# The first projection of a two-block network on one core: order of the modulation vector's copies, loads in flight, parts of the contraction, and which engine keeps the partial sums

## Chip, cores and metric

One core of a Trainium2 chip runs the whole program in one launch. The metric is device time in microseconds (us), lower is better. The times of the kernel before are three runs; the profile is one more execution.

## What is computed

Two transformer blocks follow each other on a sequence of 256 tokens with 2048 channels, in fp32. The change lies in the start of the first:

```python
mod = jax.nn.silu(c) @ w_ada[l] + b_ada[l]
shift1, scale1, gate1, shift2, scale2, gate2 = jnp.split(mod, N_MOD, axis=-1)
h = rms_norm(x, norm1_w[l]) * (1.0 + scale1[:, None]) + shift1[:, None]
proj = h @ w_in[l]
u_pool, q, k, v, g_a, g_b = jnp.split(proj, split_at, axis=-1)
```

`c` is one vector of 2048, `w_ada` is 2048 x 12288, `w_in` 2048 x 8192. Column k of `h` (128 channels, 16 such columns) can be made only when 128 values of `scale1` and 128 of `shift1` are known, and each of these groups of 128 costs one product of a 1 MB piece of `w_ada` with `c`. So the first projection needs 32 such products, and contracts over column k once column k is there.

## The kernel before

**Stream of blocks.** All weights of the large products pass as *blocks* of 1 MB (`raw`, 128 x 4 x 512 floats): four *units*, each 128 contraction rows by 512 output columns. A block has two halves of two units. For each half ScalarE rounds to fp32r (`hi`, L201), VectorE subtracts to get the rest (`lo`, L209), and TensorE makes per unit and per half of the tokens three matmuls of 512 columns (hi x hi L303, lo x hi L304, hi x lo L305): 24 matmuls a block. Four buffers hold `hi`, four `lo`, four `raw`. `Net.run` prepares halves three ahead of the one whose matmuls it issues; a half's `hi` waits until TensorE has finished the half four before it.

**Modulation products.** `ada_product` (L177) multiplies one 1 MB piece of `w_ada` with `cb` (silu(c) on all partitions) and sums along the row, on VectorE: one column of `mod`. Pieces stand in the same queue as the blocks; `pump` keeps at most `ADAB` = 2 loaded and not yet used. `prep_hi` takes the products and calls that stand ahead of a block just before that block's first `hi`.

**Start.** `setup` copies c in, applies silu and spreads it by four fp32 matmuls (L495) over four PSUM tiles. `block1` then, for each of two token halves, takes the sum of squares on ScalarE (L541), the reciprocal root (`rstd`, L335 to L340), and scales x on VectorE (L543); after the first half VectorE copies the four PSUM tiles to `cb` (L546). x is turned by 32 transposes (L555) with eight copies on ScalarE (L556).

**A column of h.** `h_tile(k)` follows the second product of column k: two one-column operations on VectorE (`sAB`, L561 and L563), then `modulate`: ScalarE writes the rounded half (L382), VectorE the full value (L383) and the difference (L384). In ScalarE's queue the next block's `hi` comes right behind L382.

**Order of the first 48 blocks.** `startup_blocks` (STARTUP = 48) orders 12 groups of 512 output columns (four of `ga`, two each of `q`, `k`, `u`, `v`) against parts of the contraction. CHUNKS = (0, 4, 10, 16): first columns 0 to 3 for all groups (blocks 0 to 11), then 4 to 9 (12 to 29), then 10 to 15 (30 to 47). `ga` 0 and 1 keep their sums in PSUM all the way; the other ten groups hold a pair of PSUM tiles (tag `acc`, four in all, two groups at a time) for one part, and `part_end` takes the sums out at the part's end: copied by ScalarE after the first part (L605), added on VectorE after the others (L607). The dictionary `when` places the products: two ahead of each of the first four blocks, then 12 from block 5 on, 1.1 blocks apart, then 12 from block 19.5 on, 1.05 apart. Behind block 47 comes `w_a_up` (its matmuls read `pT`).

Of the kernel before, what the change touches and what calls it, by code (L numbers as in the profile page):

```python
# [8 lines left out]
F32 = mybir.dt.float32  # L9
# [4 lines left out]
AF = mybir.ActivationFunctionType  # L14
# [4 lines left out]
P = 128  # L19
D = 2048  # L20
# [9 lines left out]
HLB = 4  # L30
LOOK = 3
ADAB = 2


_PK = {}
# [10 lines left out]
class Seg:  # L46
# [5 lines left out]
    def __init__(self, lhs, ks, end=None, tag="acc", end_tt=None, tail=2):  # L52
        self.lhs, self.ks, self.end, self.tag, self.end_tt = lhs, list(ks), end, tag, end_tt
        self.tail = tail if end_tt else 0
        self.acc = None
        self.left = [len(self.ks)] * 2


def lag(n):
# [4 lines left out]
class Net:  # L64
# [92 lines left out]
    def pump(self):  # L157

        while self.q_dma < len(self.queue):
            kind, what, src = self.queue[self.q_dma]  # L160
            if kind == "w":
                if what - self.prepped // 2 >= RAWB:
                    return
                t = self.rawp.tile([P, 4, 512], F32, tag="raw", name="raw")
                self.nc.sync.dma_start(out=t, in_=src)
                self.raw[what] = t
            elif kind == "a":
                if len(self.ada_dma) - self.ada_done >= ADAB:
                    return
                t = self.adap.tile([P, D], F32, tag="ada", name="ada")  # L170
# [122 lines left out]

    def unit(self, seg, k, hi, lo, tts=(0, 1)):
        if seg.acc is None:
            seg.acc = [self.psp.tile([P, 512], F32, tag=seg.tag, name="acc") for _ in range(2)]
        for tt in tts:
            first = seg.left[tt] == len(seg.ks)
            seg.left[tt] -= 1
            last = seg.left[tt] == 0  # L300
            xh, xl = seg.lhs(k, 0, tt), seg.lhs(k, 1, tt)
            a = seg.acc[tt]
            self.nc.tensor.matmul(a, xh, hi, start=first, stop=False)  # L303
            self.nc.tensor.matmul(a, xh, lo, start=False, stop=False)  # L304
            self.nc.tensor.matmul(a, xl, hi, start=False, stop=last)  # L305
# [176 lines left out]
    def setup(self):  # L482
# [22 lines left out]
        self.mask = self.t2([P, P], name="mask")  # L505
        nc.sync.dma_start(out=self.mask, in_=A["mask"])
# [5 lines left out]
        nc.vector.memset(self.eps, EPS)  # L512
        self.mod1 = fix.tile([P, 96], F32, tag="mod1", name="mod1")
        self.mod2 = fix.tile([P, 96], F32, tag="mod2", name="mod2")

    def setup2(self):
        nc, fix = self.nc, self.fix
# [8 lines left out]
    def block1(self):  # L526
# [13 lines left out]
        for tt in range(2):  # L540
            nc.scalar.activation(junk, x[:, tt, :], AF.Square, accum_out=tot[:, tt:tt + 1])  # L541
            r = self.rstd(tot[:, tt:tt + 1], 1, D)
            nc.vector.tensor_scalar(out=x[:, tt, :], in0=x[:, tt, :], scalar1=r, scalar2=None, op0=ALU.mult)  # L543
            if tt == 0:
                for i, ps in enumerate(self.cbps):
                    nc.vector.tensor_copy(self.cb[:, i * 512:(i + 1) * 512], ps)  # L546
        nc.vector.scalar_tensor_tensor(out=wb, in0=self.pk("b_ada", 16, 16), scalar=1.0, in1=self.pk("norm1_w"),
                                       op0=ALU.add, op1=ALU.mult)
        xT = mp.tile([P, KD, S], F32, tag="B", name="xT")

        for tt in range(2):
            for c in range(4):
                ps = self.ms([P, 4, P])
                for i in range(4):
                    nc.tensor.transpose(ps[:, i, :], x[:, tt, (4 * c + i) * P:(4 * c + i + 1) * P], self.ident)  # L555
                nc.scalar.copy(xT[:, 4 * c:4 * c + 4, tt * P:(tt + 1) * P], ps)  # L556
        self.at(6, self.setup2)
# [68 lines left out]
        chunk = {}  # L626
        ch = CHUNKS

        when = {}
        for c, (b0, every) in enumerate(((5, 1.1), (19.5, 1.05)), 1):  # L630
            for i in range(2 * (ch[c + 1] - ch[c])):
                when.setdefault(int(b0 + every * i), []).append((ch[c] + i // 2, i % 2))
        for nb, bl in enumerate(startup_blocks()):
            if nb < ch[1]:
                need(nb)
            for k, i in when.get(nb, ()):
                self.add_ada(ada[16 * i + k])
                if i:
                    self.add_call(lambda k=k: h_tile(k))
            units = []  # L640
            for key, k in bl:
                c = max(i for i in range(len(ch)) if ch[i] <= k)
                if key not in held and (key, c) not in chunk:
                    chunk[key, c] = Seg(h_lhs, range(ch[c], ch[c + 1]), part_end(key, c))
# [791 lines left out]


STARTUP = 48
CHUNKS = (0, 4, 10, 16)


def startup_blocks():
# [4 lines left out]
    for c in range(len(ch) - 1):  # L1447
# [2 lines left out]
            out += [(g, k) for k in ks for g in keys[:4]]  # L1450
            rest = keys[4:]
        else:
            rest = [keys[i] for i in (2, 3, 4, 0, 5, 1, 6, 8, 7, 9, 10, 11)]
        out += [(g, k) for g in rest for k in ks]
    return [out[i:i + 4] for i in range(0, len(out), 4)]

# [96 lines left out]
```

## Time and profile before

| | before |
|---|---|
| median of 3 runs | 2519.35 us (2519.08 to 2520.38) |
| profiled execution | 2517.71 us |
| its span | 2515.9 us |
| busy: TensorE, VectorE, ScalarE | 2484.1, 1807.1, 1266.9 us |
| DMA, mean over the span | 263 GB/s |
| chain that ended last | TensorE 89%, VectorE 7%, ScalarE 3% |

The profile names PE (TensorE matmuls), PEld (weight loads), DVE (VectorE), ACT (ScalarE) and SP (the engine that issues DMAs). Times in it count from the start of the span. In a timeline, the bracket behind a row is the engine's idle time just before it and what ended that. A busy TensorE can still be waiting between modelled ends, and a few per cent of its matmul records are missing.

### The profile page before, as it was taken

Reading aid. Unit: us, or ns where it says so; the run is one execution under the profiler, and the core shown is the slowest. Engines: PE = TensorE matmul, PEld = TensorE weight load, DVE = VectorE, ACT = ScalarE, POOL = GpSimd, SP = SyncE. Lnnn points to the kernel's source line nnn. Section 1 sums busy time; section 2 is a strip of 40 time slices with the busy share of each in tenths; the row PEclk is TensorE's granted clock in tenths of the full one; section 3 lists DMA queues with packets and bytes.
Section 4 is the critical chain, followed back from the end, with each engine's and each line's share of the span. In section 5 each row is a group of like instructions: output and inputs, shape, how many; then the busy total and the mean of one; then the engine's idle time right before and its main releaser. Section 6 shows DMA issues by size and latency. Waiting matters only on the chain.

```text
span 2515.9 us, 29325 instructions
## 1 busy us (share of the span) xinstructions
PE 2484.1 (99%) x11392; PEld 2053.3 (82%) x11392; DVE 1807.1 (72%) x2122; ACT 1266.9 (50%) x1739; POOL 4.0 (0%) x8
## 2 busy tenths in 40 slices
PE   8999999999999999999999999999999999999999
PEld 5878888887888888888887888888788888888887
DVE  7897888888866677787778878766676655446554
ACT  5536545445545544534446556665554453453443
POOL 0000000000000000000000000000000000000000
PEclk9999999999999999999999999999999999999999
DMA  9988678977877777787776655665567655555553
GB/s 360 376 324 317 245 298 321 397 279 280 308 311 291 305 303 301 283 334 301 301 268 228 248 219 200 234 231 193 212 252 280 258 196 199 186 184 188 192 192 130
DMA packets 92876, 662.02 MB, mean 263 GB/s; under 512 B 10689, under 2 KB 11329, under 8 KB 12737
## 3 DMA queue, kind: packets, MB, share of 16 engines
q1 hardware_dynamic: 92738, 660.16, 69.3%
q8 instruction: 89, 1.46, 0.2%
q14 instruction: 49, 0.40, 0.0%
HBM read 655.92 MB, written 4.19 MB: 262 GB/s over the span
## 4 chain that ended last, share of the span: by engine, by line
PE 89%; DVE 7%; ACT 3%; issue 1%; DMA 1%; SPq 0%; ACTq 0%; DVEq 0%
PE acc L303 28%; PE acc L305 28%; PE acc L304 28%; DVE lo L209 2%; DVE ada L177 2%; PE ms L348 1%; ACT hi L201 1%; PE ms L1176 1%; PE ms L853 1%; PE ms L1290 0%; ACT hm L1394 0%; DMA raw<-in_win 0%; PE ms L1408 0%; PE ms L359 0%; PE ms L760 0%
## 5 line engine op out<-in xcount | busy, mean ns | idle before, releaser
L209 DVE TENSOR_TENSOR lo<-raw,hi 128x1024 fp32r<-128x1024 f32 x848 | 1027.4, 1223 | 600.0 <-ACT hi L201 597.0
L201 ACT CAST hi<-raw 128x1024 fp32r<-128x1024 f32 x848 | 884.1, 1051 | 857.4 <-PE acc L305 820.8
L303 PE MATMUL acc<-hi,act 128*128 128x512 f32 x2208 | 876.6, 397 | 6.5 <-ACT hi L201 5.4
L304 PE MATMUL acc<-lo,act 128*128 128x512 f32 x2208 | 864.6, 392 | 9.3 <-DVE lo L209 9.2
L305 PE MATMUL acc<-hi,act 128*128 128x512 f32 x2208 | 863.5, 391 | 0.0
L304 PEld LDWEIGHTS acc<-lo,act 128*128 128x128 f32 x2208 | 416.4, 189 | 98.8 <-DVE lo L209 16.9
L303 PEld LDWEIGHTS acc<-hi,act 128*128 128x128 f32 x2208 | 416.1, 188 | 92.1 <-ACT hi L201 7.3
L305 PEld LDWEIGHTS acc<-hi,act 128*128 128x128 f32 x2208 | 415.7, 188 | 87.6 <-DVE act L1399 0.7
L177 DVE CUSTOM_DVE_ANT_0 ada<-ada,cb 128x2048 f32<-128x2048 f32 x192 | 438.1, 2283 | 0.0
L303 PE MATMUL acc<-hi,f 128*128 128x512 f32 x1024 | 399.6, 390 | 0.0
L305 PE MATMUL acc<-hi,f 128*128 128x512 f32 x1024 | 398.8, 389 | 0.0
L304 PE MATMUL acc<-lo,f 128*128 128x512 f32 x1024 | 398.8, 389 | 0.0
L305 PEld LDWEIGHTS acc<-hi,f 128*128 128x128 f32 x1024 | 192.3, 188 | 39.9
L304 PEld LDWEIGHTS acc<-lo,f 128*128 128x128 f32 x1024 | 192.3, 188 | 39.6
L303 PEld LDWEIGHTS acc<-hi,f 128*128 128x128 f32 x1024 | 192.3, 188 | 39.3
L382 ACT ACTIVATE act<-xT,sAB 128x256 fp32r<-128x256 f32 x16 | 9.6, 602 | 89.2 <-DVE sAB L563 89.2
L417 ACT ACTIVATE relu<-acc 128x512 f32<-128x512 f32 x64 | 37.8, 590 | 29.0 <-PE acc L305 29.0
L350 DVE TENSOR_TENSOR f<-ms,f 128x512 fp32r<-128x512 f32 x64 | 41.0, 683 | 3.7 <-ACT f L349 3.7
L393 DVE TENSOR_TENSOR res<-acc,gate 128x512 f32<-128x512 f32 x32 | 22.0, 688 | 28.2 <-PE acc L305 28.2
L396 ACT ACTIVATE res<-x 128x512 f32<-128x512 f32 x24 | 15.2, 633 | 52.5 <-DVE x L394 52.5
L418 ACT ACTIVATE relu<-relu 128x512 f32<-128x512 f32 x64 | 40.5, 633 | 2.0
L349 ACT CAST f<-ms 128x512 fp32r<-128x512 f32 x64 | 34.4, 589 | 13.7 <-PE ms L348 13.7
(245 smaller groups left out, 1291.1 us busy)
## 6 DMA issues: line engine op xcount, KB each, us to landing
raw<-in_ff SPq DMA_DIRECT2D x240, 1024.0 KB, 5.7
ada<-in_ada SPq DMA_DIRECT2D x192, 1024.0 KB, 5.7
raw<-in_win SPq DMA_DIRECT2D x120, 1024.0 KB, 6.8
raw<-in_ff1p SPq DMA_DIRECT2D x16, 1024.0 KB, 5.5
raw<-in_wa SPq DMA_DIRECT2D x8, 1024.0 KB, 6.9
raw<-in_wb SPq DMA_DIRECT2D x8, 1024.0 KB, 8.6
raw<-in_wop SPq DMA_DIRECT2D x8, 1024.0 KB, 6.8
raw<-in_wo SPq DMA_DIRECT2D x8, 1024.0 KB, 8.5
```

Of the source, the lines that this page charges most:

```text
L177: self.nc.vector.tensor_tensor_reduce(out=t, in0=t, in1=cb(), scale=1.0, scalar=0.0, op0=ALU.mult, op1=ALU.add, accum_out=mod[:, j:j + 1])
L201: self.nc.scalar.copy(hi, src)
L209: self.nc.vector.tensor_tensor(out=lo, in0=src, in1=hi.bitcast(F32), op=ALU.subtract)
L303: self.nc.tensor.matmul(a, xh, hi, start=first, stop=False)
L304: self.nc.tensor.matmul(a, xh, lo, start=False, stop=False)
L305: self.nc.tensor.matmul(a, xl, hi, start=False, stop=last)
L348: nc.tensor.transpose(ps[:, i, :], src[:, i * P:(i + 1) * P], self.ident)
L349: nc.scalar.copy(dst[:, :, 0, :], ps)
L350: nc.vector.tensor_tensor(out=dst[:, :, 1, :], in0=ps, in1=dst[:, :, 0, :].bitcast(F32), op=ALU.subtract)
L417: nc.scalar.activation(r, acc[tt], AF.Relu)
L418: nc.scalar.activation(r, r, AF.Square)
L853: mm = lambda *a, **kw: nc.tensor.matmul(*a, skip_group_check=True, **kw)
```

## The change

All of it acts on blocks 0 to 47.

- **Start.** `cb`'s first two tiles are copied ahead of x's first half being scaled, the other two behind it. The second half of x is scaled on ScalarE in four pieces, between the copies of the transposes. The load of `mask` moves from `setup` into block 2, `setup2` from half 6 to half 10.
- **Loads.** The first five modulation loads are issued without waiting for a product; three use buffers of `h`'s pool (`ADAX` = 3).
- **A column of h.** The two one-column operations go to ScalarE. From column 1 on ScalarE also makes the full value and its rounded copy; VectorE keeps the subtraction.
- **Parts.** CHUNKS = (0, 3, 8, 16): part 0 is blocks 0 to 8, part 1 blocks 9 to 23, part 2 blocks 24 to 47. Products: two ahead of each of blocks 0 to 2, then 10 from block 3 on, one a block, and 16 from block 13 on, 0.92 blocks apart; the last stands ahead of block 26 (before: 31). Part 2 begins with `ga` 2 and 3 together.
- **Partial sums.** At the end of part 1 ScalarE copies them out too, and each group's accumulators of part 1 are first filled by ScalarE from the part 0 sums (`back`, `Seg.init`), as soon as the group two before has ended (`heir`).

```diff
+ADAX = 3
...
+    def open(self, net):
+        self.acc = [net.psp.tile([P, 512], F32, tag=self.tag, name="acc") for _ in range(2)]
+        if self.init:
+            self.init(self.acc)
...
-                if len(self.ada_dma) - self.ada_done >= ADAB:
+                n = len(self.ada_dma)
+                if n >= ADAX + ADAB and n - self.ada_done >= ADAB:
                     return
...
-            first = seg.left[tt] == len(seg.ks)
+            first = seg.left[tt] == len(seg.ks) and not seg.init
...
             seg.end(seg.acc)
+            if seg.heir:
+                seg.heir.open(self)
...
+        copy_cb(0)
+        copy_cb(1)
+        scale_of(0)
+        nc.vector.tensor_scalar(out=x[:, 0, :], in0=x[:, 0, :], scalar1=r[0], scalar2=None, op0=ALU.mult)
+        copy_cb(2)
+        copy_cb(3)
+        scale_of(1)
...
+        for c in range(4):
+            turn(0, c)
+            xc = x[:, 1, c * 512:(c + 1) * 512]
+            nc.scalar.activation(xc, xc, AF.Copy, scale=r[1])
+        for c in range(4):
+            turn(1, c)
...
-            nc.vector.tensor_scalar(out=sAB[:, 0:1], in0=mod[:, 16 + k:17 + k], scalar1=self.pk("norm1_w", k, 1),
-                                    scalar2=wb[:, k:k + 1], op0=ALU.mult, op1=ALU.add)
-            nc.vector.tensor_tensor(out=sAB[:, 1:2], in0=mod[:, k:k + 1], in1=self.pk("b_ada", k, 1), op=ALU.add)
-            self.modulate(xT[:, k, :], get(k // 4)[:, k % 4, :, :], sAB[:, 0:1], sAB[:, 1:2])
+            sa, sb = sAB[:, 0:1], sAB[:, 1:2]
+            src, dst = xT[:, k, :], get(k // 4)[:, k % 4, :, :]
+            nc.scalar.activation(sa, mod[:, 16 + k:17 + k], AF.Identity, bias=wb[:, k:k + 1],
+                                 scale=self.pk("norm1_w", k, 1))
+            nc.scalar.activation(sb, mod[:, k:k + 1], AF.Identity, bias=self.pk("b_ada", k, 1))
+            if k == 0:
+                self.modulate(src, dst, sa, sb)
+                return
+            h = self.t2([P, S], name="hm")
+            nc.scalar.activation(h, src, AF.Identity, bias=sb, scale=sa)
+            nc.scalar.copy(dst[:, 0, :], h)
+            nc.vector.tensor_tensor(out=dst[:, 1, :], in0=h, in1=dst[:, 0, :].bitcast(F32), op=ALU.subtract)
...
-                    if c == 0:
+                    if c < len(ch) - 2:
                         nc.scalar.copy(d[:, tt, :], acc[tt])
...
+        def back(key):
+            def init(acc):
+                d = part(key)
+                for tt in range(2):
+                    nc.scalar.copy(acc[tt], d[:, tt, :])
+            return init
...
-        for c, (b0, every) in enumerate(((5, 1.1), (19.5, 1.05)), 1):
+        for c, (b0, every) in enumerate(((3, 1.0), (13, 0.92)), 1):
...
+                    if 0 < c < len(ch) - 2:
+                        seg.init = back(key)
+                        order[-3].heir = seg
...
-CHUNKS = (0, 4, 10, 16)
+CHUNKS = (0, 3, 8, 16)
```

How the instructions stand now, at three places. First VectorE's queue at the start of the program, from the first scaling or copy to the first product (x_99 is x, the ISA row is a product). Before:

```order
L543 TENSOR_SCALAR x_99<-x_99,rstd 128x2048
L546 COPY cb<-ms 128x512 x4
L335 TENSOR_SCALAR rstd<-sstot 128x1
L337 SCALAR_TENSOR_TENSOR rstd<-rstd 128x1
L338 TENSOR_TENSOR rstd<-rstd 128x1
L340 SCALAR_TENSOR_TENSOR rstd<-rstd 128x1
L543 TENSOR_SCALAR x_99<-x_99,rstd 128x2048
L547 SCALAR_TENSOR_TENSOR wb<-pkt 128x16
L177 ISA ada,mod_113<-ada,cb 128x2048
```

Now:

```order
L563 COPY cb<-ms 128x512 x2
L352 TENSOR_SCALAR rstd<-sstot 128x1
L354 SCALAR_TENSOR_TENSOR rstd<-rstd 128x1
L355 TENSOR_TENSOR rstd<-rstd 128x1
L357 SCALAR_TENSOR_TENSOR rstd<-rstd 128x1
L579 TENSOR_SCALAR x_99<-x_99,rstd 128x2048
L563 COPY cb<-ms 128x512 x2
L352 TENSOR_SCALAR rstd<-sstot 128x1
L354 SCALAR_TENSOR_TENSOR rstd<-rstd 128x1
L355 TENSOR_TENSOR rstd<-rstd 128x1
L357 SCALAR_TENSOR_TENSOR rstd<-rstd 128x1
L583 SCALAR_TENSOR_TENSOR wb<-pkt 128x16
```

The second scaling of x has left VectorE's queue, and the first product (L191) now follows `wb` directly; the copies of `cb` stand in two pairs.

Second, ScalarE's queue around columns 0 and 1 of h (`act` is h's tile, `hm` its full value, `hi` a block's rounded half). Before:

```order
L556 COPY xT_141<-ms_184 128x4x128
L382 ACTIVATE act_215<-xT_141,sAB_212 128x256
L201 CAST hi_220<-raw_202 128x1024
L201 CAST hi_224<-raw_202 128x1024
L382 ACTIVATE act_215<-xT_141,sAB_236 128x256
L201 CAST hi_243<-raw_210 128x1024
L201 CAST hi_247<-raw_210 128x1024
```

Now:

```order
L573 COPY xT_116<-ms_185 128x4x128
L598 ACTIVATE sAB_215<-mod1_111,wb_113,pkt_102 128x1
L600 ACTIVATE sAB_215<-mod1_111,pkt_102 128x1
L399 ACTIVATE act_216<-xT_116,sAB_215 128x256
L215 CAST hi_223<-raw_203 128x1024
L215 CAST hi_227<-raw_203 128x1024
L598 ACTIVATE sAB_237<-mod1_111,wb_113,pkt_102 128x1
L600 ACTIVATE sAB_237<-mod1_111,pkt_102 128x1
L605 ACTIVATE hm_240<-xT_116,sAB_237 128x256
L606 CAST act_216<-hm_240 128x256
L215 CAST hi_244<-raw_209 128x1024
L215 CAST hi_248<-raw_209 128x1024
```

Ahead of block 1's first `hi` one ScalarE instruction stood behind the products; now four do.

Third, the place where groups `ga` 2 and `ga` 3 end part 1. Before it was on VectorE (`gap` is their sum in SBUF; the two `lo` are block 19's):

```order
L209 TENSOR_TENSOR lo_1015<-raw_898,hi_1013 128x1024
L607 TENSOR_TENSOR gap_424<-acc_829,gap_424 128x512
L607 TENSOR_TENSOR gap_424<-acc_830,gap_424 128x512
L607 TENSOR_TENSOR gap_433<-acc_837,gap_433 128x512
L607 TENSOR_TENSOR gap_433<-acc_838,gap_433 128x512
L209 TENSOR_TENSOR lo_1035<-raw_898,hi_1033 128x1024
```

Now it is on ScalarE, in block 15's preparation (`raw_790` is block 15, `acc_893` and `acc_905` open groups `q` 0 and `k` 0 of part 1):

```order
L605 ACTIVATE hm_877<-xT_116,sAB_874 128x256
L606 CAST act_793<-hm_877 128x256
L215 CAST hi_881<-raw_790 128x1024
L648 COPY gap_382<-acc_641 128x512
L648 COPY gap_382<-acc_642 128x512
L671 COPY acc_893<-qk_427 128x512
L671 COPY acc_894<-qk_427 128x512
L648 COPY gap_391<-acc_683 128x512
L648 COPY gap_391<-acc_684 128x512
L671 COPY acc_905<-qk_427 128x512
L671 COPY acc_906<-qk_427 128x512
L215 CAST hi_909<-raw_790 128x1024
```

Four additions between two `lo` of VectorE have become eight copies between two `hi` of ScalarE, behind column 9's four instructions.

## Rows read from the trace of the kernel before

**Rows 1.** The page's first line.

```profile
span 2515.9 us, 29325 instructions
```

**Rows 2.** Busy time by stretch: us, then PE, PEld, DVE, ACT, POOL, PEclk, DMA share, GB/s.

```profile
20.00:40.00 20.00, 14.97 (x49) 10.93 (x49) 17.67 (x24) 7.10 (x9) 0.00 (x0) 0.83 0.93 365
40.00:60.00 20.00, 18.88 (x73) 14.69 (x74) 18.62 (x25) 8.33 (x11) 0.00 (x0) 0.91 0.98 404
```

**Rows 3.** Timeline of DVE, 69 to 84 us: start, length, instruction, idle before.

```profile
69.51 2.29 DVE L177 CUSTOM_DVE_ANT_0 ada<-ada,cb 128x2048 f32<-128x2048 f32 x1
71.84 0.27 DVE L561 TENSOR_SCALAR sAB<-mod,pkt,wb 128x1 f32<-128x1 f32 x1
73.79 1.22 DVE L209 TENSOR_TENSOR lo<-raw,hi 128x1024 fp32r<-128x1024 f32 x1 [0.52 <-ACT hi L201]
75.71 1.23 DVE L209 TENSOR_TENSOR lo<-raw,hi 128x1024 fp32r<-128x1024 f32 x1 [0.69 <-ACT hi L201]
76.85 2.29 DVE L177 CUSTOM_DVE_ANT_0 ada<-ada,cb 128x2048 f32<-128x2048 f32 x1
79.06 2.35 DVE L209 TENSOR_TENSOR lo<-raw,hi 128x1024 fp32r<-128x1024 f32 x2
```

**Rows 4.** Timeline of ACT over the same place.

```profile
72.22 0.60 ACT L382 ACTIVATE act<-xT,sAB 128x256 fp32r<-128x256 f32 x1 [5.30 <-DVE sAB L563]
72.72 1.04 ACT L201 CAST hi<-raw 128x1024 fp32r<-128x1024 f32 x1
73.67 1.06 ACT L605 COPY qk<-acc 128x512 f32<-128x512 f32 x2
74.61 1.06 ACT L201 CAST hi<-raw 128x1024 fp32r<-128x1024 f32 x1
```

**Rows 5.** Groups by line and form, 0 to 260 us: count | busy us, mean ns | idle before.

```profile
L177 DVE CUSTOM_DVE_ANT_0 ada<-ada,cb 128x2048 f32<-128x2048 f32 x35 | 79.6, 2284 | 0.0
...
L761 ACT ACTIVATE qkT<-ms,wq 128x512 f32<-128x512 f32 x4 | 2.6, 699 | 0.0
```

**Rows 6.** Chain of waits, us and length: last wait in blocks 0 to 47, and their end.

```profile
191.80 0.50 PE acc L304
...
317.47 0.28 PE acc L303
```

**Rows 7.** Timeline of PE, first and fourth of four successive matmuls at full clock.

```profile
28.16 0.39 PE L303 MATMUL acc<-hi,act 128*128 128x512 f32 x1
...
28.84 0.39 PE L303 MATMUL acc<-hi,act 128*128 128x512 f32 x1
```

**Rows 8.** Timeline of DVE at the start, 13 to 22 us.

```profile
13.37 1.29 DVE L543 TENSOR_SCALAR x<-x,rstd 128x2048 f32<-128x2048 f32 x1
14.66 2.29 DVE L177 CUSTOM_DVE_ANT_0 ada<-ada,cb 128x2048 f32<-128x2048 f32 x1
16.87 2.29 DVE L177 CUSTOM_DVE_ANT_0 ada<-ada,cb 128x2048 f32<-128x2048 f32 x1
21.21 1.23 DVE L209 TENSOR_TENSOR lo<-raw,hi 128x1024 fp32r<-128x1024 f32 x1 [0.51 <-ACT hi L201]
```

**Rows 9.** Timeline of ACT at the start: two one-column operations, and the last copies of x.

```profile
8.00 0.29 ACT L334 ACTIVATE rstd<-sstot,eps 128x1 f32<-128x1 f32 x1
8.32 0.20 ACT L336 ACTIVATE rstd<-rstd 128x1 f32<-128x1 f32 x1
...
12.68 0.59 ACT L556 COPY xT<-ms 128x512 f32<-128x512 f32 x1 [1.70 <-PE ms L555]
...
17.03 1.74 ACT L556 COPY xT<-ms 128x512 f32<-128x512 f32 x3 [0.27 <-PE ms L555]
```

**Rows 10.** Timeline of DVE, 207 to 211 us: the end of block 31's splits.

```profile
207.37 1.28 DVE L607 TENSOR_TENSOR v<-acc,v 128x512 f32<-128x512 f32 x2
208.57 3.49 DVE L209 TENSOR_TENSOR lo<-raw,hi 128x1024 fp32r<-128x1024 f32 x3
```

More of the change, by code (lines that the diff above doesn't have):

```diff
@@ L167, in pump @@
             elif kind == "a":
-                if len(self.ada_dma) - self.ada_done >= ADAB:
+                n = len(self.ada_dma)
+                if n >= ADAX + ADAB and n - self.ada_done >= ADAB:
                     return
-                t = self.adap.tile([P, D], F32, tag="ada", name="ada")
+                if n < ADAX:
+                    t = self.actp.tile([P, D], F32, tag="act", name="ada")
+                else:
+                    t = self.adap.tile([P, D], F32, tag="ada", name="ada")
                 self.nc.sync.dma_start(out=t, in_=src)
@@ L295, in unit @@
         if seg.acc is None:
-            seg.acc = [self.psp.tile([P, 512], F32, tag=seg.tag, name="acc") for _ in range(2)]
+            seg.open(self)
         for tt in tts:
-            first = seg.left[tt] == len(seg.ks)
+            first = seg.left[tt] == len(seg.ks) and not seg.init
             seg.left[tt] -= 1
@@ L302, in unit @@
             a = seg.acc[tt]
-            self.nc.tensor.matmul(a, xh, hi, start=first, stop=False)
-            self.nc.tensor.matmul(a, xh, lo, start=False, stop=False)
-            self.nc.tensor.matmul(a, xl, hi, start=False, stop=last)
+            mm = lambda *o, **kw: self.nc.tensor.matmul(a, *o, skip_group_check=bool(seg.init), **kw)
+            mm(xh, hi, start=first, stop=False)
+            mm(xh, lo, start=False, stop=False)
+            mm(xl, hi, start=False, stop=last)
             if last and seg.end_tt:
@@ L504, in setup @@
         nc.sync.dma_start(out=self.pkt, in_=A["pk"])
-        self.mask = self.t2([P, P], name="mask")
-        nc.sync.dma_start(out=self.mask, in_=A["mask"])
         self.ident, self.tri = (self.cst[:, i, :] for i in range(2))
@@ L514, in setup, with load_mask @@
         self.mod2 = fix.tile([P, 96], F32, tag="mod2", name="mod2")
+    def load_mask(self):
+        self.mask = self.t2([P, P], name="mask")
+        self.nc.sync.dma_start(out=self.mask, in_=self.A["mask"])
     def setup2(self):
@@ L539, in block1 @@
         junk = mp.tile([P, D], F32, tag="u", name="junk")
-        for tt in range(2):
-            nc.scalar.activation(junk, x[:, tt, :], AF.Square, accum_out=tot[:, tt:tt + 1])
[L542 to L546, printed above, removed]
+        xT = mp.tile([P, KD, S], F32, tag="B", name="xT")
@@ new lines, in block1, with copy_cb, scale_of, turn @@
+        r = {}
+        def copy_cb(i):
+            nc.vector.tensor_copy(self.cb[:, i * 512:(i + 1) * 512], self.cbps[i])
+        def scale_of(tt):
+            nc.scalar.activation(junk, x[:, tt, :], AF.Square, accum_out=tot[:, tt:tt + 1])
+            r[tt] = self.rstd(tot[:, tt:tt + 1], 1, D)
+        def turn(tt, c):
+            ps = self.ms([P, 4, P])
+            for i in range(4):
+                nc.tensor.transpose(ps[:, i, :], x[:, tt, (4 * c + i) * P:(4 * c + i + 1) * P], self.ident)
+            nc.scalar.copy(xT[:, 4 * c:4 * c + 4, tt * P:(tt + 1) * P], ps)
@@ L547, in block1 @@
+        copy_cb(0)
[5 more added lines that the diff above has]
+        scale_of(1)
         nc.vector.scalar_tensor_tensor(out=wb, in0=self.pk("b_ada", 16, 16), scalar=1.0, in1=self.pk("norm1_w"),
                                        op0=ALU.add, op1=ALU.mult)
[L549 to L556, printed above, removed]
@@ L622, in part_end @@
             return end
+        def back(key):
[4 more added lines that the diff above has]
+            return init
         held = {("ga", g): Seg(h_lhs, range(16), lambda acc, g=g: gate_a(g, acc), "ms") for g in range(2)}
         w = A["win1"]
-        chunk = {}
+        chunk, order = {}, []
         ch = CHUNKS
         when = {}
-        for c, (b0, every) in enumerate(((5, 1.1), (19.5, 1.05)), 1):
+        for c, (b0, every) in enumerate(((3, 1.0), (13, 0.92)), 1):
             for i in range(2 * (ch[c + 1] - ch[c])):
@@ L643, in block1 @@
                 if key not in held and (key, c) not in chunk:
-                    chunk[key, c] = Seg(h_lhs, range(ch[c], ch[c + 1]), part_end(key, c))
+                    seg = chunk[key, c] = Seg(h_lhs, range(ch[c], ch[c + 1]), part_end(key, c))
+                    order.append(seg)
+                    if 0 < c < len(ch) - 2:
+                        seg.init = back(key)
+                        order[-3].heir = seg
                 units.append((held[key] if key in held else chunk[key, c], k))
@@ L1452, in startup_blocks @@
         else:
-            rest = [keys[i] for i in (2, 3, 4, 0, 5, 1, 6, 8, 7, 9, 10, 11)]
+            out += [(g, k) for k in ks for g in keys[2:4]]
+            rest = [keys[i] for i in (0, 4, 1, 5, 6, 8, 7, 9, 10, 11)]
         out += [(g, k) for g in rest for k in ks]
```

5 lines of the change are left out of this document (4 added, 1 removed).

## The prediction

> **What bounds the kernel now.** The page first: the profiled execution took 2517.71 us, its span is 2515.9 us [rows 1], so 1.8 us lie around it, and it stands 1.64 us below the median of 2519.35. The chain that ended last is TensorE for 89%; so a change of blocks 0 to 47 counts only where TensorE waits there, and what it loses or gains there is carried to the end one to one.
>
> Next the chain of waits, read for the last place where TensorE waits in these blocks: 191.80 us, the second matmul of block 28 (behind the 57th split) [rows 6]. From there to the first matmul of `w_a_up` at 317.47 TensorE has no gap. Its matmuls start 0.227 us apart (0.68 for three) [rows 7], so a block of 24 costs 5.44. From 191.80 there are 23 matmuls of block 28 (5.2) and 19 blocks (103.4): 108.6 of 125.7. The other 17.1 are transposes and pooling, in both kernels.
>
> Before that place VectorE sets the pace. Its products never find it idle (idle before them 0.0 over 35) [rows 5], so no product waits for its load. What VectorE does wait for is one step, repeated for each column of h: from the second product's end at 71.80 (2.29 from 69.51) to the first split at 73.79 are **1.99 us** [rows 3]: two one-column operations, ScalarE's L382, ScalarE's `hi` of 1.04 [rows 4], then the split. Two splits back to back take 2.27 (2.35 by the row, from which the overlap of one instruction with the next, 0.08, goes) [rows 3], a product 2.21 (14.66 to 16.87) [rows 8].
>
> **A sum to test this on.** VectorE's queue from the first split at 21.21 [rows 8] to the end of block 31's, the last that has a product ahead: 32 pairs of splits 72.6, the 30 products left 66.2, 15 steps 29.9, 20 additions of part 1 at 0.60 (1.20 for two) 12.0. That gives 201.9; the trace has 209.8 (208.57 and one split) [rows 10]. The sum leaves out 7.9, of which some 0.7 at a time is ScalarE putting two copies between the two `hi` of a block (idle 0.69) [rows 3, 4].
>
> **The change in the same sum.** Now the last product stands ahead of block 26.
>
> *Start.* The first product moves from 14.66 to about 13.0: x's second scaling (1.29, 1.20 apart) goes, and c's first copies fill time in which VectorE waited. But the first split hangs on ScalarE: it now has twelve operations of about 0.5 from 12.68 on (four scalings between eight copies; the copies stand 0.58 apart or less [rows 9]), to about 18.9, then two one-column operations and L399, and its first `hi` starts near 20.3. First split at 21.4 against 21.21: the 1.7 us won on VectorE are not passed on.
>
> *The step per column.* Four ScalarE operations now follow the product instead of two on VectorE and one on ScalarE. Neither the one-column form with pointers nor the plain copy of 256 is in the trace. For the first I take 0.29 (an operation with one pointer) [rows 9] and bound it by 0.20 (no pointer) and 0.60 (L382, two pointers, 256 elements [rows 4]). For the copy 0.39, between 0.20 and 0.58 [rows 9]. From start to start: 0.04 handover, 0.28, 0.32 (the next one needs its result, as 8.00 to 8.32 [rows 9]), 0.63, 0.30, then `hi` 1.04 and 0.03: **2.64**, bounds 2.1 and 3.2. What leaves VectorE here, some 1.7 us a column, lay inside the 1.99 and frees nothing.
>
> *Parts of 3+5+8 and the denser products.* 27 pairs of splits 61.3 instead of 72.6. The additions of part 1 (12.0) are gone from VectorE.
>
> *Copies on ScalarE.* A group's end in part 1 costs four copies there instead of two additions: 20 more out, 20 in. Out of PSUM they stand 0.47 apart (0.94 for two) [rows 4]; into PSUM nothing is shown, I take the same, with 0.70 (L761) [rows 5] as the upper end. By ScalarE's order they fall between the two `hi` of a block whose column step has just held VectorE up in blocks 4, 10 and 19 (four copies), 15 (eight), 8 and 24 (two). Each delays the second split by copies + 0.95 (`hi` to the next instruction) - 1.14 (the split meanwhile): 3 x 1.69 + 3.57 + 2 x 0.75 = 10.1.
>
> *Sum.* 21.4 + 61.3 + 66.2 + 15 x 2.64 (39.6) + 10.1 = **198.6** for the end of block 26's splits. TensorE then still has 11 matmuls of that half (2.5), 21 blocks (114.2) and the 17.1: 133.8. I add 1.5 because block 24 cannot open `ga` 3 until group `v` 1 has been copied out behind two more `hi`, so that TensorE arrives late at block 26. Blocks 0 to 47 end at 333.9 instead of 317.47: +16.4. Break-even is 317.47 - 133.8 = 183.7; after splits, products and start (148.9) that leaves 34.8, or **2.32 us per column for step and copies together**; I count 3.3.
>
> *Clock.* In 20 to 40 us TensorE was granted 0.83 on average, in 40 to 60 us 0.91 [rows 2], that is 6.8 and 3.6 us at the lower of its two levels, after stretches in which it waited for splits. With waits of 4 to 7 us ahead of blocks 3, 14 and 24 I expect this to return there; only part falls where TensorE is the bound: +1.5.
>
> *The rest.* Five loads in flight: nothing, no product waited (cover: VectorE's own queue; without it a load takes its place). On SP the sixth load waits until four products are done, and block 2 waits behind it, several us before its `hi`. The mask: 64 KB less ahead of the first loads, nothing.
>
> Together **+18 us**: 2535.7 on the profiled execution's scale, **2537** on the median's.
>
> One rule of the skill speaks against the move. By the Trainium skill, "ScalarE: Activation LUTs", Rules for kernel authors, adds and multiplies belong on VectorE. By that rule the step stays at 1.99 and the sum is 9.8 us lower; the rows agree that this step got no cheaper, though it is VectorE that has no idle time. The same page, What ACT_TABLE_LOAD costs, gives 186 ns plus 0.833 ns an element, 93 ns a pointer operand and 93 ns of overlap; my estimate from that is 1.45 for the four operations, against 1.53 in the sum above, 1 us less in all.
>
> **Rivals.**
> - *The copies are covered* (12%). ScalarE waits 5.3 us for VectorE ahead of a column [rows 4], so copies might fit there; against it stands that ScalarE's queue is in order and they come behind the column. Then 188.5 + 133.8 = 322.3: +4.8, 2524.
> - *Faster: the column step is no longer than before* (7%). Place: between second product and first split. If ScalarE's four operations run within 1.99 and no copy is in the way, the sum is 148.9 + 29.9, less 1.7 if the early start is passed on: 177.1, -6.6, 2513. It decides at 2.32 per column. For it: ScalarE is idle when the product ends, and 12 us of additions go. Against: four dependent operations for one.
> - *The clock costs more* (13%). Each of three long waits followed by a low stretch as long as the longer one of rows 2, on the path: 3 x 3.4 = +10 on the forecast, 2547.
> - *Nothing to measure* (4%): the pieces cancel, within 5 us of 2519.
>
> **How the numbers follow.** The forecast (64%) has its own range of 2530 to 2545: 15 columns by the likely error of the step (0.3 either way, 4.5), copies into PSUM at 0.70 (0.23 on the 8 among those counted, 2), the rest the clock. The wide bounds of the step, 2.1 and 3.2, reach to 2529 and 2546. For 8 in 10 I go down to 2523, which takes in the covered copies and leaves out the faster case and nearly all of no change, and up to 2550. About 0.2% (5 us) is what a measurement can tell from no change. Slower by more: the forecast, the clock and half of the covered copies, 0.83. Same: the other half and the 4%, 0.10. Faster 0.07.
>
> **What would show it.** Right: VectorE idle ahead of the first split of each column of about 2.6 (0.5 before), waiting for `hi`; ScalarE's `hi` waiting for VectorE's products for the most part still; TensorE waiting some 4 to 7 us ahead of blocks 3, 14 and 24 for accumulators that ScalarE has yet to copy; the last wait near 200 us, and `w_a_up` near 335. Wrong: a step of 2.3 or less; copies found outside the pairs of `hi`; products that start after idle time, which would mean that the loads matter after all.

## The result and the profile after

The changed kernel takes **2538.36 us** (median of 4 runs, 2538.02 to 2538.86) against 2519.71 for the kernel before, run beside it (4 runs, 2519.08 to 2520.38): a ratio of 1.0074, 95% interval 1.0060 to 1.0087. It is 18.65 us slower. The forecast was 2537, range 2523 to 2550. The profiled execution took 2538.25 us; its first line answers to [rows 1]:

```profile
span 2536.5 us, 29342 instructions
```

The span is 20.6 us longer, and the chain of waits shows where. Start, length and what of it, from 180 us to the end of blocks 0 to 47, as [rows 6]:

```profile
180.02 2.28 DVE ada L191
182.34 0.33 SPq L185
182.76 6.87 DMA raw<-in_win
189.71 1.04 ACT hi L215
190.75 0.49 ACT v L648
191.29 52.03 PE acc L317 x228
...
337.38 6.87 PE acc L317 x30
```

`w_a_up` begins at 337.38 instead of 317.47: 19.9 of the 20.6 us arose in blocks 0 to 47. From 191.29 on TensorE is the chain without a gap. Just ahead of that stands something the prediction did not have: a product (`ada`), then an issue on SP that it released, then 6.87 us of a block's load, then `hi`, then the copy of `v` 1 that opens the accumulators for `ga` 3 in block 24. The place is the one named in the prediction, but what ended last there is a load, for which ScalarE had waited 0.64 us.

VectorE's timeline at one column, as [rows 3] (start, length, instruction, idle before it and what ended that):

```profile
98.68 2.29 DVE L191 CUSTOM_DVE_ANT_0 ada<-ada,cb 128x2048 f32<-128x2048 f32 x1
102.68 0.43 DVE L607 TENSOR_TENSOR act<-hm,act 128x256 fp32r<-128x256 f32 x1 [1.71 <-ACT act L606]
103.64 2.36 DVE L223 TENSOR_TENSOR lo<-raw,hi 128x1024 fp32r<-128x1024 f32 x2 [0.53 <-ACT hi L215]
```

ScalarE over the same place, as [rows 4]:

```profile
101.01 0.39 ACT L598 ACTIVATE sAB<-mod,wb,pkt 128x1 f32<-128x1 f32 x1 [6.08 <-DVE mod L191]
101.30 0.28 ACT L600 ACTIVATE sAB<-mod,pkt 128x1 f32<-128x1 f32 x1
101.61 0.60 ACT L605 ACTIVATE hm<-xT,sAB 128x256 f32<-128x256 f32 x1
102.25 0.41 ACT L606 CAST act<-hm 128x256 fp32r<-128x256 f32 x1
102.56 2.00 ACT L215 CAST hi<-raw 128x1024 fp32r<-128x1024 f32 x2
```

The product ends at 100.97 (98.68 + 2.29), the first split starts at 103.64: **2.67 us per column**, where it was 1.99 [rows 3]. ScalarE had been idle for 6.08 us before; the chain of dependent instructions, not its load, makes the step long.

Block 15's copies on ScalarE:

```profile
123.72 1.04 ACT L215 CAST hi<-raw 128x1024 fp32r<-128x1024 f32 x1
124.67 1.06 ACT L648 COPY gap<-acc 128x512 f32<-128x512 f32 x2
125.62 1.12 ACT L671 COPY acc<-qk 128x512 f32<-128x512 f32 x2
126.66 1.08 ACT L648 COPY gap<-acc 128x512 f32<-128x512 f32 x2
127.61 1.14 ACT L671 COPY acc<-qk 128x512 f32<-128x512 f32 x2
128.65 1.07 ACT L215 CAST hi<-raw 128x1024 fp32r<-128x1024 f32 x1
```

Eight copies, 0.5 apart, stand between the two `hi` of the block, just behind a column; VectorE waits 3.73 us there for the second `hi`:

```profile
129.75 1.22 DVE L223 TENSOR_TENSOR lo<-raw,hi 128x1024 fp32r<-128x1024 f32 x1 [3.73 <-ACT hi L215]
```

Last, TensorE's clock (columns as in [rows 2]):

```profile
20.00:40.00 20.00, 14.48 (x48) 10.52 (x48) 14.97 (x16) 8.06 (x14) 0.00 (x0) 0.83 0.75 291
40.00:60.00 20.00, 16.50 (x57) 12.82 (x58) 15.95 (x15) 11.55 (x18) 0.00 (x0) 0.83 0.93 366
100.00:120.00 20.00, 16.30 (x59) 12.22 (x58) 15.53 (x17) 8.95 (x14) 0.00 (x0) 0.83 0.85 329
120.00:140.00 20.00, 15.91 (x64) 12.74 (x63) 11.99 (x12) 13.37 (x25) 0.00 (x0) 0.91 0.81 317
180.00:200.00 20.00, 16.56 (x65) 12.43 (x64) 14.83 (x16) 10.29 (x18) 0.00 (x0) 0.91 0.92 378
```

These come to 27.6 us at the lower level (twice the missing share of each 20 us, since that level is half), against 10.4 before [rows 2].

### The profile page after: what moved, and what is told of

The parts are those of the page before. It is cut to its first block, busy times and chain, and to the rows that moved or that the text cites. A ratio compares the mean times of both kernels' runs of the same rounds, so it can differ in the third digit from the quotient of the medians.

```text
span 2536.5 us, 29342 instructions
## 1 busy us (share of the span) xinstructions
PE 2492.7 (98%) x11392; PEld 2057.7 (81%) x11392; DVE 1783.1 (70%) x2054; ACT 1302.6 (51%) x1828; POOL 4.0 (0%) x8
## 4 chain that ended last, share of the span: by engine, by line
PE 89%; DVE 5%; ACT 4%; issue 2%; DMA 0%; DVEq 0%; SPq 0%; ACTq 0%
PE acc L317 83%; DVE lo L223 2%; DVE ada L191 2%; PE ms L365 1%; ACT hi L215 1%; PE ms L1230 1%; PE ms L907 1%; PE ms L1344 0%; ACT hm L1448 0%; PE ms L376 0%; PE ms L512 0%; DVE res L410 0%; PE ms L814 0%; PE ms L858 0%; DMA raw<-in_win 0%
## 5 line engine op out<-in xcount | busy, mean ns | idle before, releaser
L317 PE MATMUL acc<-hi,act 128*128 128x512 f32 x4416 | 1411.6, 395 | 20.8 <-ACT hi L215 9.1
L317 PE MATMUL acc<-hi,f 128*128 128x512 f32 x2048 | 634.4, 389 | 0.0
L191 DVE CUSTOM_DVE_ANT_0 ada<-ada,cb 128x2048 f32<-128x2048 f32 x192 | 438.2, 2284 | 0.0
L317 PE MATMUL acc<-hi,pT 128*128 128x512 f32 x128 | 42.8, 399 | 0.0
L317 PE MATMUL acc<-hi,oT 128*128 128x512 f32 x128 | 40.7, 391 | 0.0
L399 ACT ACTIVATE act<-ms,shiftc,sA 128x256 fp32r<-128x256 f32 x36 | 20.3, 563 | 39.0 <-DVE hm L400 32.9
L598 ACT ACTIVATE sAB<-mod,wb,pkt 128x1 f32<-128x1 f32 x16 | 6.2, 390 | 64.2 <-DVE mod L191 64.2
L365 PEld LDWEIGHTS ms<-cst,relu 128*128 128x128 f32 x256 | 29.8, 140 | 4.2
```

What stands on the lines that cost most here:

```text
L191: self.nc.vector.tensor_tensor_reduce(out=t, in0=t, in1=cb(), scale=1.0, scalar=0.0, op0=ALU.mult, op1=ALU.add, accum_out=mod[:, j:j + 1])
L317: mm = lambda *o, **kw: self.nc.tensor.matmul(a, *o, skip_group_check=bool(seg.init), **kw)
L365: nc.tensor.transpose(ps[:, i, :], src[:, i * P:(i + 1) * P], self.ident)
```

## The experiments

"Against before" is the ratio to the kernel before, run beside each version (its medians there lie between 2519.2 and 2519.6), with its 95% interval. Times within a run are those of its profiled execution.

### Parts of the change, taken back or made alone

**The column of h as before** (in the changed kernel, `h_tile`):

```
-            nc.scalar.activation(sa, mod[:, 16 + k:17 + k], AF.Identity, bias=..., scale=...)
-            nc.scalar.activation(sb, mod[:, k:k + 1], AF.Identity, bias=...)
...
+            nc.vector.tensor_scalar(out=sAB[:, 0:1], ..., op0=ALU.mult, op1=ALU.add)
+            nc.vector.tensor_tensor(out=sAB[:, 1:2], ..., op=ALU.add)
+            self.modulate(xT[:, k, :], get(k // 4)[:, k % 4, :, :], sAB[:, 0:1], sAB[:, 1:2])
```

> The changed kernel (2538.4 us) with the columns of h made as before: two one-column operations and the full value on VectorE, one ScalarE operation. Step theory: the step from a column's second product to its first split falls from 2.68 to 1.99, 15 times 0.69 = 10 us, so 2528, with TensorE's waits ahead of blocks 3, 14 and 24 shorter but there. Density theory (products packed into 27 blocks are the cost): no more than 3 us of it goes, 2535 or above. Clock theory (the low level after waits is the cost): 2538 less at most half of the 27 us spent at the low level before 200 us, and only if the waits vanish.

Measured: 2536.06 (2532.13 to 2538.25, 4 runs), against before 1.0063 (1.0050 to 1.0077): 2.3 us below the changed kernel, where the step alone would give some 10. So the step theory, as it stood, fell here; the time lies where the density theory had it (2535 or above). Its chain of waits, the pieces of a load:

```profile
34.27 8.07 DMA raw<-in_win
...
106.05 8.22 DMA raw<-in_win
...
178.64 8.00 DMA raw<-in_win
```

Three loads of blocks are now on the chain with 24.3 us, where the changed kernel has one of 6.87; ScalarE itself waited 9.6 us for loads instead of 3.9. Each was issued on SP only when a product had released the modulation load ahead of it, and behind each of them TensorE waits at the opening of accumulators (5.7, 6.9 and 2.7 us). The clock took a part too. The last of these waits ends at 188.32, 3.0 us earlier than the 191.29 of the changed kernel, but the same 228 matmuls behind it take 2.8 us longer than the 52.03 there, at a granted clock of 0.88 from 188.32 to 215 us (1.00 in the changed kernel from 191.30 on):

```profile
188.32 54.87 PE acc L317 x228
```

(The profiled execution is the slowest of the four; the fastest, 2532.13, was granted 0.996 over the whole program instead of 0.993.)

**Part-1 sums added on VectorE** (the copies back into PSUM taken out):

```
-                    if c < len(ch) - 2:
+                    if c == 0:
...
-                    if 0 < c < len(ch) - 2:
-                        seg.init = back(key)
-                        order[-3].heir = seg
```

> The changed kernel with part 1's sums added on VectorE as before, no copies back into PSUM. If ScalarE's copies between the two roundings are a cost of 10 us and the 20 additions one of 12, as the prediction's sum has them, it gets slightly slower: 2540 to 2546. If the copies are the main cause of the loss, it gets faster by about 10: 2528.

Measured: 2549.43 (2548.24 to 2550.29), against before 1.0118 (1.0104 to 1.0132), 11.1 us above the changed kernel and more than the sum had said (2540 to 2546). The copies on ScalarE, dear as they are between two `hi`, are a gain within this change: the additions cost VectorE more. The sum had taken too much off for the copies. VectorE's idle time before splits up to block 26, apart from the 0.52 of each column, is still 6.6 us here, against 10.6 in the changed kernel, so that 4 us go and not 10, while the additions come on top; block 26's splits end at 209.89 instead of 202.05. TensorE's last wait ends 9.7 us later, and behind it, at a granted clock of 0.73 from 200 to 205 us and 0.93 from 205 to 210, the 228 matmuls take 1.6 us longer than in the changed kernel:

```profile
200.99 53.61 PE acc L317 x228
```

**Parts of 4+6+6 as before**, with the order and the product places of before:

```
-CHUNKS = (0, 3, 8, 16)
+CHUNKS = (0, 4, 10, 16)
-        for c, (b0, every) in enumerate(((3, 1.0), (13, 0.92)), 1):
+        for c, (b0, every) in enumerate(((5, 1.1), (19.5, 1.05)), 1):
-            out += [(g, k) for k in ks for g in keys[2:4]]
-            rest = [keys[i] for i in (0, 4, 1, 5, 6, 8, 7, 9, 10, 11)]
+            rest = [keys[i] for i in (2, 3, 4, 0, 5, 1, 6, 8, 7, 9, 10, 11)]
```

> The changed kernel with parts of 4+6+6, the order of blocks and the places of the products as before (last product ahead of block 31). Step theory alone: five more blocks to spread the products over take 5 pairs of splits more but give TensorE 5 blocks to run meanwhile, so about 9 us come back: 2529. If the parts do nothing, 2538.

Measured: 2529.89 (2529.11 to 2531.08), against before 1.0042 (1.0027 to 1.0058): 8.5 us less than the changed kernel, as expected. Products spread over 31 blocks instead of 26 leave VectorE more time per block.

**The column's operations on ScalarE alone** (`h_tile` of the change in the kernel before; the first edit of this section with + and - exchanged).

> The kernel before with the columns of h on ScalarE alone (four operations there, one subtraction on VectorE). Step theory: 15 times 0.69 us on the queue that sets the pace, 10 us, so 2529 or up to 3 us less where TensorE did not wait. If VectorE's relief of 1.3 us a column were worth anything: 2519 or less.

Measured: 2527.78 (2527.09 to 2528.41, 6 runs), against before 1.0031 (1.0019 to 1.0043), 8.2 us slower than before, as the step theory said (2529 or up to 3 us less): 15 columns by 0.68 would be 10.2.

**The new start and five loads alone** (in the kernel before: copies of c first, x's second scaling on ScalarE, the mask later, `ADAX = 3`).

> The kernel before with the new start alone: c copied ahead, x's second half scaled on ScalarE, five loads in flight, the mask's load moved. Both theories: nothing, 2519.7 within 1 us, since no product waits for a load and the first split waits for ScalarE; the first split at 21.2 to 21.5 us. If the loads or the start matter: 2 us or more either way.

Measured: 2517.85 (2517.12 to 2518.79, 11 runs), against before 0.9993 (0.9984 to 1.0002). Not told apart from nothing. The first split came at 20.58 us, earlier than expected: with the columns still made on VectorE the new start does bring 0.6 us, and with the columns on ScalarE alone the first split came at 21.86, 0.6 later than before. In the changed kernel the two cancel.

**Two loads in flight** (in the changed kernel):

```
-                n = len(self.ada_dma)
-                if n >= ADAX + ADAB and n - self.ada_done >= ADAB:
+                if len(self.ada_dma) - self.ada_done >= ADAB:
```

> The changed kernel with two modulation loads in flight instead of five at the start. All theories: nothing, 2538.4 within 1 us, no product found waiting for its load. If the five loads help the first blocks: 2 us or more slower.

Measured: 2541.02 (2539.02 to 2542.28), against before 1.0083 (1.0068 to 1.0098), 2.7 us above the changed kernel, where all theories had said nothing. With denser products the extra loads are worth a little. About half of it is the clock (0.89 from 190 to 215 us): the last wait ends at 192.60 instead of 191.29, and the 228 matmuls behind it take 53.30 us instead of 52.03.

### The step taken off the path

If VectorE's step per column were all, moving it behind the block's splits would give it all back. A third kind of entry in the queue does that: the column's operations are kept until the block's second split has been issued.

```
+                elif kind == "l":
+                    self.late.append(what)
...
         if half:
             del self.raw[b]
+            while self.late:
+                self.late.pop(0)()
...
-                    self.add_call(lambda k=k: h_tile(k))
+                    self.queue.append(("l", lambda k=k: h_tile(k), None))
```

**In the changed kernel:**

> The changed kernel with one thing moved: the four ScalarE operations and the subtraction of a column stand behind the roundings and splits of the block that the column's second product precedes, not ahead of them. Nothing is computed differently. Step theory: VectorE no longer waits 2.68 us per column, 15 times at least 2.2 us, and copies find ScalarE free; VectorE's own work for a pair of blocks with one column is then 9.4 us against TensorE's 10.9, so TensorE sets the pace from block 3 on and only the first three blocks wait: about 2507, faster than both kernels. Density and clock theories: no gain beyond 3 us, 2535 or more.

Measured: 2524.38 (2522.55 to 2525.63, 10 runs), against before 1.0017 (1.0007 to 1.0026): 14.0 us less than the changed kernel, not 31. The density theory, which had said no gain beyond 3, is out as the whole cause; the step theory is some 17 us short. Who waited for what in 0 to 335 us (us in total, times, longest):

```profile
ACT hi L218 <- DMA raw<-in_win: 42.8, 15, 6.6
```

In the changed kernel this wait was 3.9 us in 3. Its chain around 100 us:

```profile
99.24 2.29 DVE ada L192
...
101.57 0.33 SPq L186
...
101.99 11.11 DMA raw<-in_win
...
113.20 1.04 ACT hi L218
```

A product ends at 101.53, SP then issues the modulation load that waited for it, and only behind that the block's load, which takes 11.11 us to land. VectorE no longer waits for columns; ScalarE waits for blocks instead.

**In the kernel before,** the same edit:

> The kernel before with the same move: a column's operations behind the block's roundings and splits. Step theory: the step of 1.99 becomes VectorE's own 1.3 us for the column's operations, about 10 us of VectorE's time less, and TensorE's 6 us of waits after block 4 mostly go: 2513 to 2516. If that step was covered in the kernel before: 2519.7.

Measured: 2516.62 (2513.82 to 2519.30, 10 runs), against before 0.9990 (0.9980 to 0.9999), about 3 us, a little less than the step theory said. Here too ScalarE waited 32.9 us for block loads in 12 waits, and TensorE 13.4 us for the first columns.

### Are the loads late by their order, or by their amount?

**Order.** On top of the column behind, a block's load may be issued ahead of a modulation load that still waits for a product (`pump`; the number of buffers stays):

```
-        while self.q_dma < len(self.queue):
-            kind, what, src = self.queue[self.q_dma]
+        held = False
+        for i in range(self.q_dma, len(self.queue)):
+            kind, what, src = self.queue[i]
+            if i in self.issued:
+                continue
...
                 if n >= ADAX + ADAB and n - self.ada_done >= ADAB:
-                    return
+                    held = True
+                if held:
+                    continue
...
+            self.issued.add(i)
```

> The changed kernel with the column's operations behind the block's roundings, and a block's load no longer held in SP's queue behind a modulation load that waits for a product (it goes ahead of it; still at most four blocks and the same number of modulation loads in flight). Theory 1 (order: the loads of blocks come late because of what stands ahead of them on SP): against 2524.4 of the version without this, 2510, between 2504 and 2517; ScalarE's waits for loads fall from 42.8 us to under 20. Theory 2 (traffic: the sixteen DMA engines carry all they can between 20 and 180 us): 2522 to 2525, the waits for loads stay.

Measured: 2514.44 (2512.84 to 2518.31, 10 runs), against before 0.9982 (0.9973 to 0.9992). That is 9.9 us less than without it. The waits, and the clock from 60 to 120 us:

```profile
ACT hi L225 <- DMA raw<-in_win: 1.7, 1, 1.7
```

```profile
60.00:80.00 20.00, 19.74 (x87) 16.00 (x87) 18.55 (x25) 16.23 (x28) 0.00 (x0) 1.00 1.01 409
80.00:100.00 20.00, 20.00 (x90) 16.56 (x89) 15.48 (x16) 13.28 (x20) 0.00 (x0) 1.00 0.95 363
100.00:120.00 20.00, 20.00 (x90) 16.30 (x89) 18.54 (x18) 15.83 (x27) 0.00 (x0) 1.00 0.98 376
```

The waits for loads went from 42.8 us to 1.7, and TensorE is busy almost throughout from 60 us on. From 20 to 180 us the DMA engines moved 385 GB/s here, against 354 without the reordering; theory 2 (they carry all they can already) is out.

**Amount.** With the column behind, in the old order, half of each modulation load:

```
-                self.nc.sync.dma_start(out=t, in_=src)
+                self.nc.sync.dma_start(out=t[:, :1024], in_=src[:, :1024])
```

> As the version with the column's operations behind the roundings, but each modulation load brings half its columns (512 KB), and VectorE multiplies that half twice, so that its time stays (the modulation is that of half the sum). Both theories of the loads: against 2524.4, 2508, between 2502 and 2516. If the loads are not the bound: 2524 to 2526.

Measured: 2523.16 (2521.70 to 2525.89, 10 runs), against before 1.0016 (1.0007 to 1.0026), 1.2 us less than with whole loads. Of the 59 MB that 32 products and 27 blocks need, 16 were gone, and it hardly helped; a block's load still stands behind the gated one. This missed the expectation that both theories of the loads shared. It speaks for order, against amount, but not cleanly: VectorE's time did not stay as planned, since two half products take 2.40 us to the next instruction where one whole takes 2.21, some 6 us over 32 products, and ScalarE's waits for loads did fall, from 42.8 to 28.7 us.

```profile
ACT hi L219 <- DMA raw<-in_win: 28.7, 10, 5.4
```

**Order without the column moved** (the same edit of `pump` in the changed kernel):

> The changed kernel with only the order of the loads on SP altered as in the run above. If VectorE's queue is what holds the changed kernel up, as the prediction has it: 2535 to 2538, at most 3 us below the changed kernel (ScalarE waited for block loads 3.9 us in its trace). If the late loads were behind the +18: 2525 or less.

Measured: 2543.19 (2541.72 to 2544.48, 4 runs), against before 1.0091 (1.0074 to 1.0107): 4.8 us **slower** than the changed kernel, where neither expectation had it. Late block loads were not what made the change slow, as far as an edit with a price of its own can show it; in the changed kernel ScalarE had waited 3.9 us for them in all. Two pieces of its chain say what the edit cost:

```profile
28.07 8.36 DMA ada<-in_ada
...
111.17 7.95 DMA ada<-in_ada
```

Blocks' loads that went ahead now delay modulation loads, and the products behind them, which VectorE's queue needs first: products waited 2.1 us for their loads, where none had waited in the changed kernel.

**Blocks 3 and 4 held back** (column behind and reordered loads; only these two blocks keep their place behind the sixth modulation load):

```
-                if what - self.prepped // 2 >= RAWB:
+                if what - self.prepped // 2 >= RAWB or (held and what in (3, 4)):
```

> As the version with the column behind and the loads reordered, but blocks 3 and 4 may not go ahead of the sixth modulation load. In that version this load landed at 37.35 us, and TensorE's first long wait (to 41.5 us, for column 2) hung on it. If the loads' order bounds the start: the load lands by 34, TensorE starts block 2 by 38.5, 2511 against 2514.4, between 2508 and 2513. If that wait only moves (to block 3 or 4, whose loads now come later): 2513 to 2517.

Measured: 2513.19 (2512.93 to 2518.74, 8 runs), against before 0.9978 (0.9967 to 0.9988). Its chain:

```profile
27.70 4.89 DMA ada<-in_ada
...
35.47 9.52 DMA raw<-in_win
...
46.67 30.13 PE acc L329 x120
```

The load landed at 32.59 as hoped, and TensorE no longer waited for block 2; but block 4's load now ends TensorE's wait at 46.67 instead of 41.52. The wait moved, and the two versions can't be told apart. Both beat the kernel before by about 0.2%, and the changed kernel by 24 to 25 us.

## Why the prediction was right

The forecast of 2537 stands 1.4 us from the measured 2538.36, and the mechanism is the one it named. That it is so close is luck in part. On the scale of the profiled execution 2535.7 was said and 2538.25 measured, 2.55 short; on the medians it looks closer only because the profile before lay 1.64 us under its median and this one 0.11 under. By its steps:

- **First split**: 21.4 said, 21.28 measured. The faster start was not passed on, as said; with the columns on VectorE it comes at 20.58 (the start alone) and 20.53 (the columns taken back), so 0.6 us of it would have been, had column 0 stayed there.
- **Step per column**: 2.64 said, 2.67 measured; over 15 columns 0.5 more. The four prices were 0.39, 0.28, 0.60 and 0.41 us. By the Trainium skill, "ScalarE: Activation LUTs", What ACT_TABLE_LOAD costs, my estimates are 0.37, 0.28, 0.59 and 0.40; the means of the trace (390, 283, 601, 405 ns) agree. From the first of the four to `hi` they took 1.55 (101.01 to 102.56), where the sum had 1.53; the 1.45 that the prediction had estimated from the Trainium skill's figures is 0.1 short, most of it because the two that need the result of the one before start 0.03 and 0.04 behind its end. The plain copy of 256, which the prediction says is not in the trace, does stand elsewhere in the trace of the kernel before (L1396, 406 ns). The Trainium skill's rule on that page, in Rules for kernel authors, that adds and multiplies belong on VectorE, points the same way for the step, which alone cost 8.2 us. The reason given there is speed per element; what counted here is the length of a chain of dependent operations. For the sums of part 1 the run points the other way: on VectorE they cost 11.1 us more than as copies on ScalarE.
- **Copies between two `hi`**: 10.1 said. By the same measure, from the six pairs of splits, 10.8 (idle 1.66, 0.69, 1.73, 3.73, 1.73 and 0.69 before the second of each). No run took these copies away without putting additions in their place.
- **Block 26's splits**: 198.6 said. In VectorE's timeline they are the first two of these four:

```profile
199.69 4.63 DVE L223 TENSOR_TENSOR lo<-raw,hi 128x1024 fp32r<-128x1024 f32 x4 [0.53 <-ACT hi L215]
```

  and end at 199.69 + 2.36 = 202.05. That is 3.4 later. The terms above explain 1.1 of it (0.5 + 0.7 - 0.1). The other 2.3 were in no term of the sum, and VectorE's timeline from the first split on shows most of them. The sum counts a product as 2.21, to the start of the next instruction, but a step from the product's end, 2.29 behind its start: 0.08 is lost at each column, 1.2 in all. Six small operations of `setup2` take 0.5, and one more wait for `hi`, before the split at 134.66, is 0.3. The test on the kernel before had the first two of these among the 7.9 that it left out, and the prediction did not carry them over. Late loads are not among them. ScalarE waited for a block's load three times (1.68, 1.53 and 0.64 us), and each time VectorE was at work meanwhile and came to the next split without idle time, as here at the 1.53:

```profile
115.36 2.28 DVE L191 CUSTOM_DVE_ANT_0 ada<-ada,cb 128x2048 f32<-128x2048 f32 x1
115.53 2.00 ACT L215 CAST hi<-raw 128x1024 fp32r<-128x1024 f32 x2 [1.53 <-DMA raw<-in_win]
117.57 2.35 DVE L223 TENSOR_TENSOR lo<-raw,hi 128x1024 fp32r<-128x1024 f32 x2
```

- **From there to the end**: 133.8 + 1.5 said; 337.38 - 202.05 = 135.3 measured. TensorE's last wait was in block 24 for the copies of `v` 1, where the 1.5 had it, and the 0.64 us for which ScalarE waited for a block's load lie on the way to it. 333.9 was said for the end, 337.38 came, and 0.7 more arose behind it.
- **Clock**: +1.5 said, on top. The low stretches did come, each at the end of a wait of TensorE or just behind it (3.3, 2.7, 2.7, 4.1 and 3.1 us long, ending at 21.30, 40.18, 113.10, 126.28 and 187.68; one of 2.6, ending at 52.37, had none), and their sum grew by 17 us. But the blocks' end is accounted for without a term for them: most of them lie where TensorE had to wait for VectorE anyway. Behind the last wait there is none here (0.228 us a matmul from 191.29 on), but 2.8, 1.6 and 1.3 us with the columns taken back, with the sums on VectorE and with two loads. No run changed the clock alone, so how much of it is on the path ahead of the last wait stays open.
- **Loads: nothing.** Wrong in size: with two loads the changed kernel takes 2.7 us more, about half of it through the clock. And "no product waited" asked too narrow a question. Products did not wait after either (idle before them 0.0 over 33); the block's load behind a gated modulation load did come late, by 3.9 us in all. The remark in brackets there, that without the cover of VectorE's queue a load takes its place, is what the column experiments then showed.

VectorE's waits show the whole as the prediction had asked for it:

```profile
L223 DVE TENSOR_TENSOR lo<-raw,hi 128x1024 fp32r<-128x1024 f32 x75 | 89.6, 1222 | 40.3 <-ACT hi L215 40.3
L191 DVE CUSTOM_DVE_ANT_0 ada<-ada,cb 128x2048 f32<-128x2048 f32 x33 | 75.0, 2285 | 0.0
```

VectorE lost 40.3 us before splits up to 260 us (24.7 in the kernel before, over 83 of them) and another 25.7 before the 15 subtractions of a column. TensorE's waits ahead of blocks 3, 14 and 24 came, for the copies named, but with 2.6, 4.1 and 3.1 us instead of 4 to 7.

Of the rivals, the covered copies fell with the 10.8, the faster case with the 2.67 per column, which alone is above the 2.32 that it allowed for step and copies together, no change and the dear clock with the time. What the experiments add is that the parts of the sum do not add up when they are taken one by one. The step alone costs 8.2 us, and all the rest without it 16.8 (the columns taken back), 25 together, where the whole change costs 18.65. Taking the parts back returned 8.5 of 9, but taking the step off returned 2.3 of 10 and 14 of 31, because a second limit, the order of SP's queue, lies a few us below the first. With the column behind, the run with reordered loads shows this limit; with the columns taken back it is read from the chain of one execution, in which the clock took a part too.

## What to carry to other kernels

A chain of small dependent operations that sits between the work of the engine that sets the pace is priced by its length on the path, product end to next split, not by which engine is idle: moving it from the busy engine to the idle one made it 0.68 us longer, 15 times. Before you count on a gain from shortening such a chain, look for the next limit: a load that shares an in-order queue with loads gated by that same work is late although a buffer is free for it. The two cures here (column behind the splits, block loads not held behind gated ones) were worth 14 and then 10 us in that order, while the second alone cost 5.

## What was not expected of the hardware

- A block's 1 MB load took 5.4 us to land in the later stages (`in_ff`, median of 240, with the column behind), but 7 to 11 us in the pieces of the chains above, where it was issued right behind another 1 MB load on the same queue; with that other load halved it was 6.5 to 10 on the chain.
- TensorE's time at its lower clock differed much between versions that had the same matmuls to do: by the granted clock in 20 to 215 us, 10.3 us before, 27.3 after, 34 with the columns taken back, with the sums on VectorE and with the order alone, and 10.2 with the column behind and the loads reordered. It was longer where TensorE waited more: its waits of over 1 us from 18 us on come to 6.1 us before, 18.4 after, 23.7 with the columns taken back and 10.0 with the loads reordered. Their count alone does not tell it: the columns on ScalarE alone had six, as the changed kernel had, but of 10.5 us together, and 13.6 us at the lower clock.
- ScalarE's copies into PSUM took no less than those out of it: 604 to 618 ns of L671 against 584 to 592 of L648.
